# A two-layer decoder trunk: the RWKV pass over all tiles at once in two staggered halves, six projection units side by side at the start, and the 256-column matmul first in every second block

## The chip, the cores and the metric

The kernel runs on one core of a Trainium2 chip. The metric is the device time of one execution in microseconds (us); the kernel before took 2397.22 us as the median of three runs (2396.86 to 2416.54). "Within 1%" of that median is 2373.2 to 2421.2 us.

## The reference, cut to what matters

The input x is 256 tokens of 2048 features, float32. Two layers follow one another, each of the form

```python
h = _rms_norm(x, norm_mix[layer])
u = h @ w_in                       # one combined input projection
y = concat(head_group_1(u), head_group_2(u)) @ w_out
x = x + y
x = x + _sq_relu_mlp(_rms_norm(x, norm_mlp[layer]), w_ff1, w_ff2)   # 2048 -> 8192 -> 2048
```

In layer 0 the head groups are a sparse attention (NSA, 8 heads) and RWKV-7 time mixing (16 heads of 64), in layer 1 a gated linear recurrence and HGRN2. The change concerns the RWKV-7 recurrence, the projection ahead of it, and the way in which all the large products are issued. RWKV-7 is a recurrence over time with a 64x64 state per head:

```python
def step(state, inp):
    r_t, w_t, k_t, v_t, a_t, b_t = inp
    sa = jnp.einsum('bhij,bhj->bhi', state, a_t)
    state = state * w_t[:, :, None, :] + sa[..., None] * b_t[:, :, None, :] + v_t[..., None] * k_t[:, :, None, :]
    return state, jnp.einsum('bhij,bhj->bhi', state, r_t)
```

## The kernel before, in words

Activations lie transposed: 128 features on the partitions, 256 tokens along the free axis, 16 such tiles for 2048 features. Float32 accuracy on TensorE is had by splitting. An activation tile `hx[k]` is 512 columns wide: 256 columns of its rounded high part and 256 of the rest (`prepare`, L192). A weight tile is split in the same way by `split` (L128): a cast on ScalarE makes `wh` (L130), a subtraction on VectorE makes `wl` (L132), eight 128x128 tiles at a time. One product of a weight tile with an activation tile, called a block here, is then two matmuls (`mm3`, L147): `wh` against all 512 columns (L152) and `wl` against the 256 high columns (L153), both into one PSUM bank. A `unit` (L156) is 16 such blocks, k = 0 to 15, for 128 output features. Where only half the columns are wanted (`folded`, the second half of the output projection) the 512-column matmul is two of 256 columns (L149, L150), so a block is three matmuls of 256 columns.

There are 48 units in each input projection (`mm_i`), 64 up and 64 down units in each MLP (`mm_f`, 4096 blocks in all), and the output projections (`mm_o`) have 256 blocks in their first and 256 in their folded halves over both layers: 6144 blocks with the 1536 of the input projections. Weights stream from memory in 512 KB pieces on SP's queue (L125).

Layer 0's mix (`layer0_mix`, L233) goes in these steps:

- The start (L251 to L288): x and the first units' weights are loaded, `hx` is made tile by tile, then units 0 and 1 run one after the other, then 2 and 3.
- `rwkv_a` (L310): the rest of units 0 to 27. For each of eight tiles j (two heads each) it forms decays, keys, values and the 64x64 pair products, and stores them to memory: `rwp_d` (128 x 2052 per tile: the vectors `a`, `r`, the transposed keys and values, the decay, the bonus and the gate) and `pm_d` (pair products). All of these DMAs are on GpSimd's queue. From `pm_d` small 32x32 pieces are gathered into `nb` (L432).
- `rw_solve` (L437): 30 steps of two VectorE operations invert these triangles; the result goes to memory as `z_d` (L448).
- `rwkv_b` (L450): four passes, for the tile pairs (0,1), (2,3), (4,5), (6,7). A pass loads `inv` from `z_d`, `pm`, `rwp` and `bg` (L466 to L470), completes the inverse with two groups of 32x32 matmuls (`psh` L478, `psf` L484), then walks four chunks of 64 tokens: `psx` (state part L494 with 128 rows and 64 columns of TensorE, pair part L496 with 64 rows), copy, `psu` (L503, 64 rows), copy, new state `pss` (L510, 128x128), output `psy` (state part L521, 128x128; value part L523). At the end of a pass come a mean (`pmn`, L529), a variance (`pvr`, L534) and the result's halves in `yr` (L543, L544). `rwp` has one buffer, so a pass's load waits for the pass before it.
- `nsa_keys` and `nsa_head` (units 28 to 47 and the attention's small matmuls `nr_q`, `s`, `t`, `o`).
- `out_proj` (L917): first the half that reads `yr`, then, folded, the half that reads `yn`.

A scheduler sorts the instructions of each engine when the program is built, with the priorities that the code sets; on the chip each engine takes its list strictly in order. It lays matmuls of NSA heads and of units between the RWKV steps.

## Time and profile before

| | |
|---|---|
| median of 3 runs | 2397.22 us |
| lowest, highest | 2396.86, 2416.54 us |
| the profiled execution | 2415.31 us, of which the span is 2413.5 us |
| granted TensorE clock, mean of the span | 0.997 |
| busy: PE, DVE, ACT, POOL | 2390.6, 1697.7, 1243.7, 44.9 us |

The profiled execution is one of the two longer ones among the four times that are known, 18.1 us above the median. PE is TensorE (PEld its weight loads), DVE VectorE, ACT ScalarE, POOL GpSimd, SP the queue that loads the weights. Matmuls are pipelined and their ends are modelled, so that the distance between the starts of two matmuls tells what one costs, and not the duration that its row gives. A float32 matmul outside the split products stands as two instructions in the trace.

### The profile page before, as it was taken

Reading aid. Unit: us, or ns where it says so; the run is one execution under the profiler, and the core shown is the slowest. Engines: PE = TensorE matmul, PEld = TensorE weight load, DVE = VectorE, ACT = ScalarE, POOL = GpSimd, SP = SyncE. Lnnn points to the kernel's source line nnn. Section 1 sums busy time; section 2 is a strip of 40 time slices with the busy share of each in tenths; the row PEclk is TensorE's granted clock in tenths of the full one; section 3 lists DMA queues with packets and bytes.
Section 4 is the critical chain, followed back from the end, with each engine's and each line's share of the span. In section 5 each row is a group of like instructions: output and inputs, shape, how many; then the busy total and the mean of one; then the engine's idle time right before and its main releaser. Section 6 shows DMA issues by size and latency. Waiting matters only on the chain.

```text
span 2413.5 us, 37947 instructions
## 1 busy us (share of the span) xinstructions
PE 2390.6 (99%) x14386; PEld 2072.1 (86%) x14386; DVE 1697.7 (70%) x3006; ACT 1243.7 (52%) x2152; POOL 44.9 (2%) x118
## 2 busy tenths in 40 slices
PE   8999999999999999999999999999999999999999
PEld 6888877798888888888888888889888888888888
DVE  7887865677676576576568888788777667667555
ACT  7554455555444444444456666675544444444443
POOL 0112010000000000000000000000000000000000
PEclk9999999999999999999999999999999999999999
DMA  7667743465555555655555444456556555656564
GB/s 263 212 216 228 246 139 105 155 209 183 190 184 186 188 184 187 188 185 187 187 176 187 150 151 153 154 168 217 185 191 191 189 188 191 192 187 190 191 199 134
DMA packets 125862, 446.77 MB, mean 185 GB/s; under 512 B 14192, under 2 KB 19952, under 8 KB 124016
## 3 DMA queue, kind: packets, MB, share of 16 engines
q1 hardware_dynamic: 115824, 414.06, 53.7%
q0 software_dynamic: 5456, 26.79, 3.1%
q10 hardware_dynamic: 4400, 3.50, 0.4%
q8 instruction: 114, 1.87, 0.3%
q14 instruction: 68, 0.56, 0.1%
HBM read 429.06 MB, written 15.22 MB: 184 GB/s over the span
## 4 chain that ended last, share of the span: by engine, by line
PE 93%; DVE 3%; DMA 2%; ACT 1%; issue 1%; POOL 0%; DVEq 0%; ACTq 0%; POOLq 0%
PE mm_f L152 39%; PE mm_f L153 20%; PE mm_i L152 13%; PE mm_i L153 7%; PE mm_o L153 2%; PE mm_o L152 1%; PE mm_o L149 1%; PE mm_o L150 1%; DVE wl_i L132 1%; PE hl L816 1%; PE pair L425 1%; DMA rwp<-rwp_d 1%; PE psx L496 0%; ACT wh_o L130 0%; PE psu L503 0%
## 5 line engine op out<-in xcount | busy, mean ns | idle before, releaser
L132 DVE TENSOR_TENSOR wl_f<-raw_f,wh_f 128x1024 fp32r<-128x1024 f32 x512 | 627.2, 1225 | 486.1 <-ACT wh_f L130 486.1
L130 ACT CAST wh_f<-raw_f 128x1024 fp32r<-128x1024 f32 x512 | 538.6, 1052 | 773.4 <-PE mm_f L152 566.8
L152 PE MATMUL mm_f<-hx_m,wh_f 128*128 128x512 f32 x2048 | 717.2, 395 | 0.0
L152 PE MATMUL mm_f<-z,wh_f 128*128 128x512 f32 x2048 | 717.1, 395 | 0.0
L152 PE MATMUL mm_i<-hx_a,wh_i 128*128 128x512 f32 x1536 | 563.9, 405 | 11.5 <-ACT wh_i L130 11.4
L153 PE MATMUL mm_f<-hx_m,wl_f 128*128 128x256 f32 x2048 | 574.8, 281 | 0.0
L153 PE MATMUL mm_f<-z,wl_f 128*128 128x256 f32 x2048 | 574.4, 280 | 0.0
L152 PEld LDWEIGHTS mm_f<-z,wh_f 128*128 128x128 f32 x2048 | 383.9, 187 | 90.0
L152 PEld LDWEIGHTS mm_f<-hx_m,wh_f 128*128 128x128 f32 x2048 | 383.9, 187 | 90.0
L153 PE MATMUL mm_i<-hx_a,wl_i 128*128 128x256 f32 x1536 | 447.6, 291 | 1.2 <-DVE wl_i L132 1.0
L153 PEld LDWEIGHTS mm_f<-hx_m,wl_f 128*128 128x128 f32 x2048 | 387.0, 189 | 0.1
L153 PEld LDWEIGHTS mm_f<-z,wl_f 128*128 128x128 f32 x2048 | 387.0, 189 | 0.0
L152 PEld LDWEIGHTS mm_i<-hx_a,wh_i 128*128 128x128 f32 x1536 | 289.8, 189 | 72.3 <-ACT wh_i L130 12.1
L153 PEld LDWEIGHTS mm_i<-hx_a,wl_i 128*128 128x128 f32 x1536 | 291.5, 190 | 9.3 <-DVE wl_i L132 4.0
L130 ACT CAST wh_i<-raw_i 128x1024 fp32r<-128x1024 f32 x192 | 201.3, 1049 | 188.9 <-PE mm_i L152 169.5
L132 DVE TENSOR_TENSOR wl_i<-raw_i,wh_i 128x1024 fp32r<-128x1024 f32 x192 | 234.5, 1222 | 80.6 <-ACT wh_i L130 76.4
L168 DVE TENSOR_TENSOR s_f<-mm_f,t_f 128x256 f32<-128x256 f32 x256 | 106.7, 417 | 3.0 <-ACT t_f L167 3.0
L132 DVE TENSOR_TENSOR wl_o<-raw_o,wh_o 128x1024 fp32r<-128x1024 f32 x64 | 78.3, 1223 | 32.6 <-ACT wh_o L130 32.3
L130 ACT CAST wh_o<-raw_o 128x1024 fp32r<-128x1024 f32 x64 | 67.2, 1050 | 63.3 <-issue 29.2
L167 ACT COPY t_f<-mm_f 128x256 f32<-128x256 f32 x256 | 93.2, 364 | 4.3 <-PE mm_f L153 4.3
L153 PE MATMUL mm_o<-ym,wl_o 128*128 128x256 f32 x256 | 72.6, 284 | 0.8 <-DVE wl_o L132 0.8
L942 DVE TENSOR_TENSOR s_f<-s_f,rstd_m 128x256 f32<-128x256 f32 x128 | 54.4, 425 | 4.4
(420 smaller groups left out, 2254.7 us busy)
## 6 DMA issues: line engine op xcount, KB each, us to landing
raw_f<-in_w_ff_dram SPq DMA_DIRECT2D x512, 512.0 KB, 4.5
raw_i<-in_w_in_dram SPq DMA_DIRECT2D x192, 512.0 KB, 4.1
raw_o<-in_w_out_dram SPq DMA_DIRECT2D x64, 512.0 KB, 4.2
rwp_d<-rwp POOLq DMA_DIRECT2D x8, 1026.0 KB, 7.1
rwp<-rwp_d POOLq DMA_DIRECT2D x4, 1540.0 KB, 10.7
cw<-in_cmp_w_dram SPq DMA_DIRECT2D x2, 2048.0 KB, 10.2
...
```

The source lines that it names most:

```text
L130: A.copy(wh, raw)
L132: V.tensor_sub(wl, raw, wh)
L149: M.matmul(ps[:, :T], wh, mv[:, :T], start=first, stop=False)
L150: M.matmul(ps[:, :T], wh, mv[:, T:], start=False, stop=False)
L152: M.matmul(ps, wh, mv, start=first, stop=False)
L153: M.matmul(ps[:, :T], wl, mv[:, :T], start=False, stop=last)
L167: A.copy(t, ps[:, T:])
L168: V.tensor_add(s, ps[:, :T], t)
L425: M.matmul(pps[q][:, c * P : (c + 1) * P], bk[hs, c], ar[hs, c], start=True, stop=True)
L816: M.matmul(pl[:, x * T + i * P : x * T + (i + 1) * P], qk[:, ii], qk[:, ii], start=True, stop=True)
L942: V.tensor_mul(s, s, rstd)
```

## The change

Three things are changed, and what follows from them.

1. **Six units at the start.** `w_in0` is laid out so that for each k the 128x128 weight tiles of units 0 to 5 lie together (768 columns, 384 KB). For each k the loop makes `hx[k]`, splits the six tiles and issues six blocks into six PSUM banks. Sixteen matmuls on a zeroed tile stand ahead of the first block. The small loads of `rw_w2`, `rw_a2` and `rw_g2` wait for the first cast (`issue_after`).
2. **RWKV in one pass.** `rwkv_b` is called once and works in two halves of four tiles (eight heads) each. Per chunk of 64 tokens and half it loads `inv` (four DMAs), `pm`, `rw` and `gb` into two buffers that both halves share, zeroes the upper rows of the values in `rw` with a memset on GpSimd, and does all steps for four tiles at once. The pair parts of `psx` and `psu` now use all 128 rows of TensorE (with zeroed rows in `xv`, `inv` and `rw`), and the parts with the state and the state's update are split by head into 64 columns. Mean and variance are taken per chunk. The two halves are generators whose steps alternate, the first one four steps ahead. `rwp_d` and `pm_d` are one tensor each, by chunk.
3. **Turned blocks.** In `unit`, and in the first half of `out_proj`, every odd k issues the `wl` matmul ahead of the `wh` matmul. Units 0 to 5 and the folded half are not turned.

```diff
+NFIRST = 6
...
-    def mm3(ps, wh, wl, mv, first, last, folded=False):
+    def mm3(ps, wh, wl, mv, first, last, folded=False, turned=False):
+        if turned:
+            M.matmul(ps[:, :T], wl, mv[:, :T], start=False, stop=False)
+            M.matmul(ps, wh, mv, start=False, stop=last)
+            return
...
-            mm3(ps, wh[:, k % 8], wl[:, k % 8], mv[k], k == 0, k == KT - 1, folded)
+            mm3(ps, wh[:, k % 8], wl[:, k % 8], mv[k], k == 0, k == KT - 1, folded, k % 2 == 1)
...
+            rwp_d = dram.tile([P, 8, 4, 512], F32, name="rwp_d")
+            pm_d = dram.tile([P, 8, 4, 2, P], F32, name="pm_d")
+            wts = mx.tile([P, 8, 4], F32, name="wts", bufs=1)
...
+                w_k = w_in0[0:NFIRST].rearrange("n p m -> (n p m)").rearrange("(k p c) -> k p c", k=KT, p=P)
+                first = [
+                    pmm.tile([P, 512], F32, tag="mm", name=f"mm_i0_{u}") if u < 2 else bank(f"mm_i0_{u}", ("ga", "gb", "gc")[(u - 2) % 3])
+                    for u in range(NFIRST)
+                ]
+                wrm = pa.tile([P, P], F32, name="wrm")
+                V.memset(wrm, 0.0)
+                pw = bank("warm", "gc")
...
+                    for k in range(KT):
+                        if k % 2 == 0:
+                            nc.sync.dma_start(xi[k // 8][:, k % 8 : k % 8 + 2], xT[:, k : k + 2])
+                        raw = wraw.tile([P, 8, P], F32, tag="raw", name=f"raw_i0_f{k}")
+                        nc.sync.dma_start(raw[:, :NFIRST], w_k[k].rearrange("p (b c) -> p b c", c=P))
+                        raws.append(raw)
+                        if k == 9:
+                            nc.sync.dma_start(con, consts)
+                    for i in range(16):
+                        M.matmul(pw[:, :P], wrm, wrm, start=True, stop=True)
...
+                    for k in range(KT):
+                        prepare(hx, k, xi[k // 8][:, k % 8], "gmix0")
+                        wh = wspl.tile([P, 8, P], F32R, tag="wh", name=f"wh_i0_f{k}")
+                        ins = A.copy(wh[:, :NFIRST], raws[k][:, :NFIRST])
+                        anchor = anchor or ins.ins
+                        wl = wspl.tile([P, 8, P], F32R, tag="wl", name=f"wl_i0_f{k}")
+                        V.tensor_sub(wl[:, :NFIRST], raws[k][:, :NFIRST], wh[:, :NFIRST])
+                        for u in range(NFIRST):
+                            mm3(first[u], wh[:, u], wl[:, u], hx[k], k == 0, k == KT - 1)
+                        if k % 4 == 3:
+                            squares(k // 4)
+                    rstd = rstd_of(acc, "a0", "gc")
+                first.append(unit(w_in0[NFIRST], hx, f"i0_{NFIRST}", tag="gb"))
+                rwkv_a(pa, gate, hx, scaled_by(rstd), rwp_d, pm_d, wts, nb, first, load_cw, anchor)
             with tc.tile_pool(name="pb", bufs=1) as pb, tc.tile_pool(name="pn", bufs=1) as pn:
                 rw_solve(pb, nb, z_d)
...
-                for j in range(0, 8, 2):
-                    rwkv_b(pb, j, rwp_d, pm_d, z_d, yr)
+                rwkv_b(pb, rwp_d, pm_d, z_d, wts, yr)
...
+        inv_ = [tl(f"inv{i}", (P, 8, 64)) for i in range(2)]
+        xv_ = [tl(f"xv{i}", (P, 4, P)) for i in range(2)]
+        s_ = [tl(f"s{i}", (P, 4, P)) for i in range(2)]
+        for t in inv_ + xv_ + s_:
+            G.memset(t, 0.0)
+        zv = z_d.rearrange("(i j c q) r t -> i c q r j t", i=2, j=8, c=4)
...
+            for i in range(2):
+                for q in range(2):
+                    G.dma_start(inv8[32 * i : 32 * i + 32, :, q, 32 * i : 32 * i + 32], zv[i, c, q, :, js])
+            pm = tl("pm", (P, 4, 2, P), 2, name=f"pmc_{n_}")
+            G.dma_start(pm, pm_d[:, js, c])
+            rw = tl("rw", (P, 4, 384), 2, name=f"rw_{n_}")
+            G.dma_start(rw, rwp_d[:, js, c, 0:384])
+            gb = tl("gb", (P, 4, 128), 2, name=f"gb_{n_}")
+            G.dma_start(gb, rwp_d[:, js, c, 384:512])
+            G.memset(rw[0:64, :, 256:384], 0.0)
...
+            psx = bank(f"psx_{n_}")
+            for r in range(4):
                 if c:
-                    M.matmul(psx[0:64, r * P : (r + 1) * P], ar[:, r, c, 0], s[:, r], start=True, stop=False)
+                    M.matmul(psx[0:64, r * P : (r + 1) * P], ac[:, r], s[:, r], start=True, stop=False)
                 for h in range(2):
-                    M.matmul(psx[0:64, r * P + h * 64 : r * P + h * 64 + 64], pm[64:128, r, 4 * h + c, 0:64],
-                             uv[64:128, r, c, h * 64 : h * 64 + 64], start=c == 0, stop=c == 0 or h == 1)
+                    M.matmul(psx[0:64, r * P + h * 64 : r * P + h * 64 + 64], pm[:, r, h, 0:64],
+                             uv[:, r, h * 64 : h * 64 + 64], start=c == 0, stop=c == 0 or h == 1)
...
+                    M.matmul(psu[0:64, r * P + h * 64 : r * P + h * 64 + 64], inv[:, 2 * r + h],
+                             xv[:, r, h * 64 : h * 64 + 64], start=True, stop=True)
...
+                    o = psy[h * 64 : h * 64 + 64, r * 64 : r * 64 + 64]
+                    if c:
+                        M.matmul(o, s[:, r, h * 64 : h * 64 + 64], rc[:, r], start=True, stop=False)
+                    M.matmul(o, uv[:, r, h * 64 : h * 64 + 64], pm[:, r, h, 64:128], start=c == 0, stop=True)
...
+                        M.matmul(pss[h * 64 : h * 64 + 64, r * 64 : r * 64 + 64],
+                                 rw[:, r, 128 + h * 64 : 128 + h * 64 + 64], uv[:, r, h * 64 : h * 64 + 64], start=True, stop=True)
...
+        halves = [chain.from_iterable(map(chunk, range(4), [b] * 4)) for b in range(2)]
+        for _ in range(4):
+            next(halves[0])
+        while halves:
+            halves = [h for h in halves if next(h, 1) is None]
...
-                        mm3(ps, wh[:, k], wl[:, k], ym[half * 8 + k], k == 0, k == 7, o == 1)
+                        mm3(ps, wh[:, k], wl[:, k], ym[half * 8 + k], k == 0, k == 7, o == 1, o == 0 and k % 2 == 1)
```

The order of the instructions, as the scheduler lays them, changes at three places on which the prediction rests. First TensorE's list inside one unit of the first MLP (`mm_f1_0_0_1` is the unit's bank, `hx_m0` the activations, `wh` and `wl` the two parts of the weights), before and after:

```order
L152 MATMUL mm_f1_0_0_1_6222<-hx_m0_0_5108,wh_f1_0_0_1_0_6225 128x512
L153 MATMUL mm_f1_0_0_1_6222<-hx_m0_0_5108,wl_f1_0_0_1_0_6227 128x256
L152 MATMUL mm_f1_0_0_1_6222<-hx_m0_0_5108,wh_f1_0_0_1_0_6225 128x512
L153 MATMUL mm_f1_0_0_1_6222<-hx_m0_0_5108,wl_f1_0_0_1_0_6227 128x256
L152 MATMUL mm_f1_0_0_1_6222<-hx_m0_0_5108,wh_f1_0_0_1_0_6225 128x512
```

```order
L159 MATMUL mm_f1_0_0_1_6370<-hx_m0_0_5256,wh_f1_0_0_1_0_6373 128x512
L160 MATMUL mm_f1_0_0_1_6370<-hx_m0_0_5256,wl_f1_0_0_1_0_6375 128x256
L152 MATMUL mm_f1_0_0_1_6370<-hx_m0_0_5256,wl_f1_0_0_1_0_6375 128x256
L153 MATMUL mm_f1_0_0_1_6370<-hx_m0_0_5256,wh_f1_0_0_1_0_6373 128x512
L159 MATMUL mm_f1_0_0_1_6370<-hx_m0_0_5256,wh_f1_0_0_1_0_6373 128x512
```

Long and short matmuls alternated before; now two short ones and two long ones follow one another, and no matmul is added or lost.

Second TensorE's list in the second chunk of an RWKV pass. Before it is the group `psx` in chunk 1 of the pair (2,3); `st` is the state, `rwp` and `pm` are what the pass loaded:

```order
L494 MATMUL psx_2_1_2850<-st_2_0_2841,rwp_2_2778 64x128
L496 MATMUL psx_2_1_2850<-rwp_2_2778,pm_2_2777 64x64 x2
L494 MATMUL psx_2_1_2850<-st_2_0_2841,rwp_2_2778 64x128
L496 MATMUL psx_2_1_2850<-rwp_2_2778,pm_2_2777 64x64 x2
```

After it is the same group in chunk 1 of the first half (`s0` is its state, `rw` and `pmc` what it loads):

```order
L522 MATMUL psx_1_0_2853<-s0_2657,rw_1_0_2805 64x128
L524 MATMUL psx_1_0_2853<-rw_1_0_2805,pmc_1_0_2803 64x64 x2
L522 MATMUL psx_1_0_2853<-s0_2657,rw_1_0_2805 64x128
L524 MATMUL psx_1_0_2853<-rw_1_0_2805,pmc_1_0_2803 64x64 x2
L522 MATMUL psx_1_0_2853<-s0_2657,rw_1_0_2805 64x128
L524 MATMUL psx_1_0_2853<-rw_1_0_2805,pmc_1_0_2803 64x64 x2
L522 MATMUL psx_1_0_2853<-s0_2657,rw_1_0_2805 64x128
L524 MATMUL psx_1_0_2853<-rw_1_0_2805,pmc_1_0_2803 64x64 x2
```

One group now serves four tiles, and there are eight such groups for the kernel instead of sixteen. Between the first `psh` and the last `pvr` TensorE's list holds, beside the RWKV matmuls, 86 blocks and some seven NSA heads before, and 28 blocks and three heads after; what left that stretch stands behind it.

Third GpSimd's list where `rwkv_a` ends (`nb` is the gathering of the triangles for `rw_solve`, `pmc`, `rw` and `gb` the loads of the first chunk of the first half, `_0_0`, and of the second, `_0_1`). Before:

```order
L462 MEMSET inv_0_2599 64x1024
L468 DMA pm_0_2601<-pm_d0_99 128x2048
L469 DMA rwp_0_2602<-rwp_d0_95 128x2x1540
L470 DMA bg_0_2603<-rwp_d0_95 128x2x512
L432 DMA nb_105<-pm_d3_102 8x32x32 x2
```

After:

```order
L498 DMA pmc_0_0_2669<-pm_d_96 128x4x256
L500 DMA rw_0_0_2671<-rwp_d_95 128x4x384
L502 DMA gb_0_0_2673<-rwp_d_95 128x4x128
L498 DMA pmc_0_1_2733<-pm_d_96 128x4x256
L503 MEMSET rw_0_0_2671 64x4x128
L500 DMA rw_0_1_2735<-rwp_d_95 128x4x384
L502 DMA gb_0_1_2737<-rwp_d_95 128x4x128
L456 DMA nb_100<-pm_d_96 8x32x32
```

The last gathering into `nb` now stands behind a memset (L503) that has to wait until the first `rw` load has landed.

## Rows read from the trace of the kernel before

**Rows 1.** The page, part 1: busy us, share of the span and instructions of each engine.

```profile
PE 2390.6 (99%) x14386; PEld 2072.1 (86%) x14386; DVE 1697.7 (70%) x3006; ACT 1243.7 (52%) x2152; POOL 44.9 (2%) x118
```

**Rows 2.** The page, part 4: the chain that ended last, shares by engine.

```profile
PE 93%; DVE 3%; DMA 2%; ACT 1%; issue 1%; POOL 0%; DVEq 0%; ACTq 0%; POOLq 0%
```

**Rows 3.** Four windows: length, busy us and (count) of PE, PEld, DVE, ACT, POOL, clock, DMA, GB/s.

```profile
575.00:1275.00 700.00, 700.00 (x3964) 607.04 (x3963) 454.31 (x646) 321.31 (x461) 0.00 (x0) 1.00 0.58 185
1725.00:2375.00 650.00, 650.00 (x3752) 573.15 (x3751) 422.39 (x590) 296.29 (x413) 0.00 (x0) 1.00 0.60 192
316.60:459.50 142.90, 142.45 (x1167) 107.44 (x1168) 82.75 (x293) 76.01 (x222) 10.55 (x15) 0.96 0.33 112
322.00:325.00 3.00, 3.00 (x16) 2.14 (x16) 0.47 (x3) 1.92 (x8) 0.00 (x0) 0.50 0.04 11
```

**Rows 4.** The timeline of PE in layer 1's MLP: start us, us, instruction.

```profile
2000.30 0.39 PE L152 MATMUL mm_f<-hx_m,wh_f 128*128 128x512 f32 x1
2000.53 0.28 PE L153 MATMUL mm_f<-hx_m,wl_f 128*128 128x256 f32 x1
2000.65 0.39 PE L152 MATMUL mm_f<-hx_m,wh_f 128*128 128x512 f32 x1
```

**Rows 5.** The timeline of PE in the folded half of the output projection.

```profile
529.86 0.28 PE L149 MATMUL mm_o<-yn,wh_o 128*128 128x256 f32 x1
529.98 0.28 PE L150 MATMUL mm_o<-yn,wh_o 128*128 128x256 f32 x1
530.10 0.28 PE L153 MATMUL mm_o<-yn,wl_o 128*128 128x256 f32 x1
```

**Rows 6.** The chain in order of time, 250 to 480 us: start, us on it, what.

```profile
316.62 1.20 PE psh L478 x32
...
324.62 1.04 PE psu L503 x8
...
347.29 12.62 DMA rwp<-rwp_d
360.04 0.65 PE psx L496 x8
...
435.27 0.44 PE pss L510 x4
435.71 0.38 PE psy L523 x8
437.02 0.37 PE psx L496 x4
...
438.86 0.60 PE psu L503 x8
...
441.63 0.36 PE psy L521 x2
...
450.87 0.36 PE psx L494 x2
...
457.61 0.87 PE pvr L534 x2
```

**Rows 7.** The timeline of all engines at the start of the kernel.

```profile
6.05 2.90 ACT L193 ACTIVATE hx_a<-xi,par 128x256 fp32r<-128x256 f32 x7 [4.04 <-DMA xi<-in_xT_dram]
...
10.92 0.80 PE L152 MATMUL mm_i<-hx_a,wh_i 128*128 128x512 f32 x1 [10.92 <-ACT wh_i L130]
...
13.20 0.63 PE L152 MATMUL mm_i<-hx_a,wh_i 128*128 128x512 f32 x1
...
13.84 0.63 PE L152 MATMUL mm_i<-hx_a,wh_i 128*128 128x512 f32 x1
```

**Rows 8.** Window from 0 to 50.3 us, line L152 alone: length, PE, PEld, clock, DMA share, GB/s.

```profile
0.00:50.30 50.30, 35.76 (x96) 18.68 (x96) 1.00 0.80 277
```

**Rows 9.** Groups by line, 0 to 25 us: busy us, mean ns | idle before, releaser.

```profile
L194 DVE SCALAR_TENSOR_TENSOR hx_a<-xi,par,hx_a 128x256 fp32r<-128x256 f32 x16 | 6.5, 480 | 6.6 <-ACT hx_a L193 6.6
...
L132 DVE TENSOR_TENSOR wl_i<-raw_i,wh_i 128x1024 fp32r<-128x1024 f32 x5 | 6.0, 1220 | 1.5 <-ACT wh_i L130 1.4
```

More of the change, by code (lines that the diff above doesn't have):

```diff
@@ L2 @@
 from contextlib import ExitStack
+from itertools import chain
 import numpy as np
@@ L54 @@
 HG_LEVELS = (1, 2, 4, 8, 16, 32)
-RWP_N = 4 * 512 + 4
+NFIRST = 6
 @with_exitstack
@@ L235, in layer0_mix @@
             acc, hx = norm("a0")
-            rwp_d = [dram.tile([P, 2, RWP_N], F32, name=f"rwp_d{j}") for j in range(4)]
-            pm_d = [dram.tile([P, 2, 8, P], F32, name=f"pm_d{j}") for j in range(4)]
+            rwp_d = dram.tile([P, 8, 4, 512], F32, name="rwp_d")
+            pm_d = dram.tile([P, 8, 4, 2, P], F32, name="pm_d")
+            wts = mx.tile([P, 8, 4], F32, name="wts", bufs=1)
             z_d = dram.tile([P, 32, 32], F32, name="z_d")
@@ L316, in shifted @@
             G.memset(ub[:, 0:1], 0.0)
-            scaled(first[u] if u < 4 else unit(w_in0[u], hx, f"i0_{u}"), ub[:, 1:], name)
+            scaled(first[u] if u < len(first) else unit(w_in0[u], hx, f"i0_{u}"), ub[:, 1:], name)
             d = tl("d", bufs=2, name=f"d_{name}")
@@ new lines, in tl, with chunk @@
+            return pb.tile(list(shape), F32, tag=tag, name=name or tag, bufs=bufs)
+        inv_ = [tl(f"inv{i}", (P, 8, 64)) for i in range(2)]
[4 more added lines that the diff above has]
+        zv = z_d.rearrange("(i j c q) r t -> i c q r j t", i=2, j=8, c=4)
+        def chunk(c, b):
+            inv, xv, s = inv_[b], xv_[b], s_[b]
+            js = slice(4 * b, 4 * b + 4)
+            n_ = f"{c}_{b}"
+            inv8 = inv.rearrange("p (j q) t -> p j q t", q=2)
+            for i in range(2):
[8 more added lines that the diff above has]
+            G.memset(rw[0:64, :, 256:384], 0.0)
+            pm8 = pm.rearrange("p j q t -> p (j q) t")
+            zat = tl(f"zat{b}", (64, 8, 32), name=f"zat_{n_}")
+            V.transpose(zat[0:32], inv[0:32, :, 0:32])
+            psh = bank(f"psh_{n_}")
+            for n in range(8):
+                M.matmul(psh[32:64, n * 32 : (n + 1) * 32], pm8[0:32, n, 32:64], zat[0:32, n], start=True, stop=True)
+            A.copy(zat[32:64].rearrange("p n t -> p (n t)"), psh[32:64, 0:256])
+            yield
+            psf = bank(f"psf_{n_}")
+            for n in range(8):
+                M.matmul(psf[0:32, n * 32 : (n + 1) * 32], zat[32:64, n], inv[32:64, n, 32:64], start=True, stop=True)
+            A.copy(inv[0:32, :, 32:64], psf[0:32, 0:256].rearrange("p (n t) -> p n t", n=8))
+            ac, rc, uv = rw[:, :, 0:64], rw[:, :, 64:128], rw[:, :, 256:384]
+            yield
+            psx = bank(f"psx_{n_}")
+            for r in range(4):
@@ L517, in rwkv_b @@
-            psy = bank(f"psy_{j}_{c}")
-            for r in R:
-                rr = slice(r * 64, r * 64 + 64)
-                if c:
-                    M.matmul(psy[:, rr], s[:, r], ar[:, r, c, 1], start=True, stop=False)
-                for h in range(2):
-                    M.matmul(psy[h * 64 : h * 64 + 64, rr], uv[:, r, c, h * 64 : h * 64 + 64], pm[:, r, 4 * h + c, 64:128],
-                             start=c == 0, stop=True)
-            A.copy(y4[:, :, c], psy[:, 0:P].rearrange("p (r t) -> p r t", r=2))
@@ L526, in rwkv_b @@
-            s = sn
-        yf = y.rearrange("p r t -> p (r t)")
-        pmn = bank(f"pmn_{j}")
-        M.matmul(pmn, bones, yf, start=True, stop=True)
-        V.scalar_tensor_tensor(yf, pmn, -1.0 / 64, yf, ALU.mult, ALU.add)
-        sq = tl("ysq", (P, 512))
-        A.activation(sq, yf, AF.Square)
-        pvr = bank(f"pvr_{j}")
-        M.matmul(pvr, bones, sq, start=True, stop=True)
-        rs = tl("ysq", (P, 512), name=f"yrs_{j}")
-        rsqrt_of(rs, pvr, 1.0 / 64, eps_ln, f"y{j}", pb)
@@ new lines, in chunk @@
+            A.copy(xv[0:64].rearrange("p r t -> p (r t)"), psx[0:64])
+            yield
+            psu = bank(f"psu_{n_}")
+            for r in range(4):
+                for h in range(2):
+                    M.matmul(psu[0:64, r * P + h * 64 : r * P + h * 64 + 64], inv[:, 2 * r + h],
+                             xv[:, r, h * 64 : h * 64 + 64], start=True, stop=True)
+            A.copy(uv[0:64], psu[0:64].rearrange("p (r t) -> p r t", r=4))
+            yield
+            psy = bank(f"psy_{n_}")
@@ new lines, in chunk @@
+            yield
+            pmn = bank(f"pmn_{n_}")
+            M.matmul(pmn[:, 0:T], bones, y, start=True, stop=True)
+            V.scalar_tensor_tensor(y, pmn[:, 0:T], -1.0 / 64, y, ALU.mult, ALU.add)
+            sq = tl(f"ysq{b}", (P, T), name=f"ysq_{n_}")
+            A.activation(sq, y, AF.Square)
+            yield
+            pvr = bank(f"pvr_{n_}")
+            M.matmul(pvr[:, 0:T], bones, sq, start=True, stop=True)
+            rs = tl(f"ysq{b}", (P, T), name=f"yrs_{n_}")
+            rsqrt_of(rs, pvr[:, 0:T], 1.0 / 64, eps_ln, f"y{n_}", pb)
```

162 lines of the change are left out of this document (54 added, 108 removed).

## The prediction, made before the result was known

> **What bounds the kernel now.** I read the busy times first, then the chain that ended last, then windows by stage, and the timeline only where two windows disagreed. TensorE is busy for 99% of the span, the next engine, VectorE, for 70% [rows 1], and 93% of the chain that ended last is TensorE [rows 2]. So time is won where TensorE does less, goes from one matmul to the next faster, or stands still less. Busy alone does not tell these apart, so I count matmuls in windows. Layer 0's MLP issues 3964 matmuls in 700 us, which is 1982 blocks of 353.2 ns; layer 1's MLP, the same code, 3752 in 650 us, which is 1876 blocks of 346.5 ns [rows 3]. The program has two paces and stays in one for a whole MLP. The difference is 6.7 ns on 2048 blocks, 13.7 us. The profiled execution took 2415.3 us (span 2413.5 and 1.8 around it), 18.1 us more than the median. With the faster pace in layer 0's MLP it would have been 2401.6, and the input projections of layer 0 have stretches of the slow pace too, so I take the median of 2397.2 for a run at the fast pace throughout. The sum is made against 2415.3, and the 18.1 is taken off at the end.
>
> The RWKV passes are the stretch with the poorest use of TensorE. From the first `psh` at 316.6 us to the end of the last `pvr` at 458.5 [rows 6] four passes follow one another, 35.5 us each. PE counts as busy in all of it, while the DMA share falls to 0.33 [rows 3]: few weights are consumed.
>
> **Turned blocks.** Nothing is added; 2896 pairs of blocks change their order (2048 in the MLPs, 42 and 48 units with 8 each in the projections, 128 in the output projections). A pair was long, short, long, short; it becomes long, short, short, long. So of each pair one step from short to long and one from long to short go, and a step from short to short and one from long to long come. The trace shows long to short as 230 ns and short to long as 120 at two digits [rows 4], and short to short as 120 in the folded half [rows 5]. Long to long it does not show. The bare columns are 213.3 and 106.7 ns at 2.4 GHz, the level that the windows at 1.00 stand for [rows 3]. Short to short is thus its columns and 13.3 ns, and a block of 346.5 is its 320.0 ns of columns and 26.5, twice the same. I therefore take each matmul to cost its columns and 13.3 ns in any order, and long to long to cost 226.7: the change is 0. The bounds are the bare 213.3 and, as far on the other side, 240: the slow pace shows that at least 6.7 ns more are possible. That is 13.3 ns either way on 2896 pairs, 38.5 us down or up.
>
> **Six units at the start.** The first block begins at 10.92 us, after half a unit of weights and eight tiles of x [rows 7]. After the change it needs one k: the first activation tile can be made at 6.05 us as now [rows 7], in 0.5 us, and the cast of 768 columns follows, 0.8 us, so 7.4. But sixteen matmuls stand ahead of it. One float32 matmul of 128 columns is 0.22 us (two `pss` take 0.44 [rows 6]) and double that at half clock, so they take some 7 us from about 1 us on: 8.0. That is 2.9 us earlier. The first blocks now go 0.64 us apart [rows 7], not 0.35; seven of them cost 2.0 us, which the sixteen matmuls take over. From then on TensorE needs 6 x 0.347 = 2.08 us per k. VectorE needs 0.48 for the activation, 0.92 for 768 of the 1024 columns of 1220 ns [rows 9], and about 0.4 for the squares, 1.8 together. The loads are 512 KB per k, 252 GB/s, and the first 50 us ran at 277 [rows 8]. Both fit with little to spare, so I give 1.9 of the 4.9 us back for misses. Now 96 blocks are reached at 50.3 us [rows 8]; the small matmuls that ran between them come later and cost what they cost. Term: -3 us, between -5 and +2.
>
> **RWKV in one pass.** The cost of TensorE's groups is read from the chain [rows 6]. Before, one chunk with a state, for two tiles: `psx` 2 x (0.36 + 0.37) = 1.46, `psu` 0.60, `pss` 0.44, `psy` 2 x 0.36 + 0.38 = 1.10, together 3.60. Chunk 0 has no state: 0.65 + 0.60 + 0.44 + 0.38 = 2.07. Chunk 3 has no `pss`: 3.16. With 2.3 for `psh` and `psf` (1.20, taken alike) and 1.75 for `pmn` and `pvr` (0.87, alike), a pass is 2.07 + 7.20 + 3.16 + 4.05 = 16.5, and four are 66 us.
>
> After, one chunk of one half serves four tiles. Four pair matmuls of `psx` in one form take 0.65 and two take 0.37 [rows 6]: 0.14 for each and 0.09 once per group. With the same form throughout, `psx` is 8 x 0.14 + 4 x 0.22 + 0.09 = 2.1 and `psu` 8 x 0.14 + 0.09 = 1.2. `psy` (16 matmuls) and `pss` (8) alternate between the two column positions as L523 does, 0.095 each: 1.5 and 0.8. `psh` and `psf` are 1.15, mean and variance 0.9. That is 7.65; chunk 0 is 6.0 and chunk 3 6.9. A half is 6.0 + 15.3 + 6.9 = 28.2, both 56.4. Term: -9.6 us. Bounds: nothing gained (all 0.14 and a switch at each group), and -17 (all at 0.095).
>
> The row for `psx` is where a rule can be weighed: two matmuls of L496 between two of L494 take 0.37, four together 0.65, so that four in pieces would take 0.74 [rows 6]. The Trainium skill, TensorEngine Tiling (Array Packing), Key Properties, says that a change of the tiling mode drains TensorE; the trace agrees in sign, with 0.09 us. By that rule the one form inside a chunk is a gain, but each NSA or projection matmul laid between the groups still pays it.
>
> The waits around this work I leave as they are: 141.9 us of wall time held 66 of RWKV work, and what else stood there (86 blocks and seven heads) moves behind the stretch, where the `yr` half of the output projection fills between the heads. What a chunk loads is new on the path. The longest load that ended the chain is 12.62 us, once [rows 6]; that wait can go, or six later chunk loads can each show 4 us of theirs, since both halves share two buffers: between -12 and +24. I take 0, because 81 us of TensorE work (56.4, 28 blocks and three heads of 5 us) stand between the groups. VectorE and ScalarE, 83 and 76 us busy in that 143 us window [rows 3], have room.
>
> The last gathering into `nb` stands behind a memset that waits for a load of the RWKV values, the like of which took 12.62 us [rows 6]. `rw_solve` starts later, while TensorE's list reaches the first `psh` 12 matmuls earlier, 12 x 0.173 = 2.1 us. Between 0 and +12; I take +2.
>
> **Sum.** 2415.3 - 3.0 - 9.6 + 2.0 = 2404.7 for the profiled pace; less 18.1, 2386.6, so 2386 us for the median.
>
> **The rivals.**
>
> *A long matmul after a long one costs its bare columns.* Then 13.3 ns go on 2896 pairs, 38.5 us: 2347. For it: the weights of the second long matmul have twice the time of the short one to arrive, and the 120 of short to short may come from them. Against it: a long matmul costs 230 though the weights of the short one that follows had the same long time [rows 4]. The opposite, 240, would be 2425.
>
> *The slow pace holds.* If the new order falls into the slow pace in one MLP, as layer 0's does here [rows 3], the median is 2386 + 13.7 = 2400. The trace shows that both occur with the same code; it does not show what chooses.
>
> *Half clock in the RWKV pass.* This is the way to a slower kernel. Inside the first pass the clock stands at 0.50 (322 to 325 us [rows 3]), when 32x32 matmuls and waits had gone before, and `psu` takes 1.04 us there and 0.60 later [rows 6], 1.7 times as long. After, the 81 us of this stretch hold only 28 blocks of full-size matmuls instead of 86. If all of it ran at half clock, 57 us more: 2443. Each us at half clock loses 0.41, so it takes 35 us of loss, 85 us at half clock, to be slower than before by over 1%. Against it: passes two to four hold the same matmuls, and the mean of all 142.9 us is still 0.96 [rows 3].
>
> **How the numbers follow.** My forecast has 0.44; its own range by the bounds above is 2362 to 2400, and about 0.13 of the 0.44 lies under 2373.2. The bare long matmul has 0.27, of which 0.25 lies under 2373.2. The slow pace has 0.16, all within 1%. Half clock, long loads in the RWKV pass, or a dearer long matmul have 0.13, of which 0.11 lies above 2421.2. A measurement here can tell about 1% from no change. So faster by over 1%: 0.38; within: 0.51; slower: 0.11. The range reaches from the first rival's 2347, with part of the RWKV gain beside it, 2338, to the slow pace with some load waits, 2412.
>
> **What would show it right or wrong.** In the windows over the two MLPs: 346.5 ns per block with turned blocks, and about 227 from long to long on the timeline. A block near 340 is the first rival, near 353 the second. The first block at 8 us, and 96 blocks by about 44. From the first `psh` to the last `pvr` 75 to 100 us; the granted clock there; `rw` loads on the chain for less than 20 us. The forecast is wrong if the MLPs' blocks change by over 3 ns, or if the RWKV stretch and what follows it, up to the first MLP matmul, do not end about 10 us earlier.

## The result and the profile after

The changed kernel took 2427.1 us (median of 7 runs, 2425.2 to 2430.4), the kernel before, run beside it, 2398.6 (7 runs); the ratio is 1.010, 95% interval 1.007 to 1.013. The forecast was 2386 us with a range up to 2412: the time is 41 us above the forecast. Runs of the kernel before stand in two groups, at about 2397 and 2411 us, a distance that fits the two paces of its MLPs [rows 3], and its profile is of the upper group; stages are therefore compared in the profiles.

The profiled execution took 2426.5 us (span 2424.7). Its stages, from the starts of TensorE's matmuls in the traces; run 1 is the first experiment below, which has the first two parts of the change without turned blocks:

| us | before | after | run 1 |
|---|---|---|---|
| start to the first matmul of layer 0's MLP | 559.0 | 540.8 | 537.7 |
| layer 0's MLP | 724.2 | 728.7 | 710.6 |
| layer 1's mix and output projection | 415.0 | 422.0 | 415.0 |
| layer 1's MLP | 710.6 | 728.7 | 710.7 |

The first row is 18 us shorter, some 4 us of which are the slower execution that was profiled before (18.1 us above the median, 13.6 of it in layer 0's MLP). Both MLPs, which only the turned blocks touch, lose the gain and more against the quick pace of 710.6. Part 1 of the page, after, still calls PE busy for 99%, as [rows 1]:

```profile
PE 2403.2 (99%) x14530; PEld 2045.1 (84%) x14530; DVE 1718.2 (71%) x3031; ACT 1260.5 (52%) x2148; POOL 70.1 (3%) x164
```

What changed stands in the idle column of part 5 (busy us, mean ns | idle us before, and what ended most of it), after:

```profile
L174 ACT COPY t_f<-mm_f 128x256 f32<-128x256 f32 x256 | 95.4, 373 | 469.0 <-PE mm_f L153 469.0
...
L160 PEld LDWEIGHTS mm_f<-hx_m,wl_f 128*128 128x128 f32 x1024 | 192.4, 188 | 86.8 <-DVE wl_f L135 47.9
...
L160 PEld LDWEIGHTS mm_f<-z,wl_f 128*128 128x128 f32 x1024 | 192.2, 188 | 52.5 <-DVE wl_f L135 2.4
```

The same lines of run 1, without turned blocks:

```profile
L160 PEld LDWEIGHTS mm_f<-hx_m,wl_f 128*128 128x128 f32 x2048 | 387.1, 189 | 0.1
...
L174 ACT COPY t_f<-mm_f 128x256 f32<-128x256 f32 x256 | 92.9, 363 | 4.3 <-PE mm_f L160 4.3
```

Two things are new. ScalarE spends 469 us waiting in front of `t_f`, the eviction copy, where it waited 4. This is a sign of another order and no loss in itself: in run 1 ScalarE waits in front of the cast `wh_f` instead, 759.0 us against 258.7 after. And the weight loads of `wl_f` in the up units (operand `hx_m`) wait 48 us for VectorE's subtraction, those of the down units (`z`) hardly at all. The eviction copies tell the time of a unit, since there is one in each: the summary of L174 in layer 1's MLP, 1740 to 1835 us (up) and 1900 to 1960 us (down), gives the first and the last start. After:

```profile
L174 ACT COPY t_f<-mm_f x16: 373/373/373, 1744.5 to 1831.5; 128x256 f32<-128x256 f32 x16
...
L174 ACT COPY t_f<-mm_f x11: 372/373/373, 1900.4 to 1956.2; 128x256 f32<-128x256 f32 x11
```

Up units stand 87.0 / 15 = 5.80 us apart (362.5 ns per block), down units 55.8 / 10 = 5.58 (348.7). From the starts of all matmuls: 5800 and 5577 ns in both layers, against 5547 for the quick pace of before (346.7 ns per block). So 128 up units lose 0.223 us to something that the down units don't meet, 28.5 us, and all 256 units lose 0.030, 7.7 us. With 7.0 us in layer 1's mix that is 43 of the 46 us between after and run 1; the other 3 stand ahead of layer 0's MLP.

The timelines show the 0.223. TensorE in an up unit of layer 1, after (H, the long matmul, is L159 or L153; L, the short one, L160 or L152; [rows 4] show plain blocks):

```profile
2004.27 0.40 PE L153 MATMUL mm_f<-hx_m,wh_f 128*128 128x512 f32 x1
2004.50 0.40 PE L159 MATMUL mm_f<-hx_m,wh_f 128*128 128x512 f32 x1
2004.85 0.38 PE L160 MATMUL mm_f<-hx_m,wl_f 128*128 128x256 f32 x1
2005.07 0.28 PE L152 MATMUL mm_f<-hx_m,wl_f 128*128 128x256 f32 x1
2005.19 0.39 PE L153 MATMUL mm_f<-hx_m,wh_f 128*128 128x512 f32 x1
```

The weight loads there:

```profile
2004.85 0.19 PEld L160 LDWEIGHTS mm_f<-hx_m,wl_f 128*128 128x128 f32 x1 [0.40 <-DVE wl_f L135]
2004.96 0.19 PEld L152 LDWEIGHTS mm_f<-hx_m,wl_f 128*128 128x128 f32 x1
2005.08 0.19 PEld L153 LDWEIGHTS mm_f<-hx_m,wh_f 128*128 128x128 f32 x1
```

ScalarE and VectorE of the same unit:

```profile
2001.91 0.37 ACT L174 COPY t_f<-mm_f 128x256 f32<-128x256 f32 x1 [1.92 <-PE mm_f L153]
2002.18 1.06 ACT L133 CAST wh_f<-raw_f 128x1024 fp32r<-128x1024 f32 x1
...
2002.32 0.42 DVE L175 TENSOR_TENSOR s_f<-mm_f,t_f 128x256 f32<-128x256 f32 x1 [1.06 <-ACT t_f L174]
2002.78 0.43 DVE L979 TENSOR_TENSOR s_f<-s_f,rstd_m 128x256 f32<-128x256 f32 x1
2003.23 0.42 DVE L980 SCALAR_TENSOR_TENSOR s_f<-s_f 128x256 f32<-128x256 f32 x1
2003.58 1.22 DVE L135 TENSOR_TENSOR wl_f<-raw_f,wh_f 128x1024 fp32r<-128x1024 f32 x1
```

The matmul at 2004.50 is the ninth block's, the first of the unit's second half. Its L comes 0.35 us later instead of 0.23, and the next L 0.22 instead of 0.12: 0.22 in all. Read backwards: the load waits for a subtraction that ends at 2004.80; that began at 2003.58 though its cast was done at 2003.24, because the three eviction instructions stand ahead of it; and the cast itself began at 2002.18, behind `t_f`, which could begin only when the unit before had ended. The engines' lists, as built, say the same. ScalarE before:

```
L130 CAST wh_f1_1_1_15_1_19376<-raw_f1_1_1_15_1_19374 128x1024
L167 COPY t_f1_1_1_14_19359<-mm_f1_1_1_14_19314 128x256
```

ScalarE after:

```
L174 COPY t_f1_1_1_14_19507<-mm_f1_1_1_14_19462 128x256
L133 CAST wh_f1_1_1_15_1_19524<-raw_f1_1_1_15_1_19522 128x1024
```

`t_f1_1_1_14` evicts unit 14, `wh_f1_1_1_15_1` is the second half of unit 15. The buffer that this cast fills holds weights of unit 14, and is free once that unit's last H has read them. Before, an L came behind that H, and the scheduler put the cast ahead of the eviction; with the sixteenth block turned, the last H is the unit's end, and the eviction goes first. It does so at all 254 places where one MLP unit follows another in a layer, and the cast goes first at all 254 before.

The down units have the same order and don't wait, since their eviction has two instructions on VectorE and not three. After:

```profile
1906.25 1.06 ACT L133 CAST wh_f<-raw_f 128x1024 fp32r<-128x1024 f32 x1
...
1906.84 0.43 DVE L987 TENSOR_TENSOR xs<-xs,s_f 128x256 f32<-128x256 f32 x1
1907.34 1.23 DVE L135 TENSOR_TENSOR wl_f<-raw_f,wh_f 128x1024 fp32r<-128x1024 f32 x1
```

VectorE is through with the eviction at 1907.27 and the cast with `wh_f` at 1907.31, so the subtraction starts 0.03 us behind its cast, where it is 0.34 us late in the up unit.

The Trainium skill, TensorE: Matmul & The Clock Gate, section LDWEIGHTS (loading the stationary operand), gives a weight load in ns as its columns over 1.2, an estimate of 107 ns for 128. The trace agrees in the spacing: the three late loads start 0.11 and 0.12 us apart, though the row of each lasts 0.19. An L's bare columns are 106.7 ns, so by that rule a short matmul has nothing to spare for the load of the one behind it, and a load that came late under one short matmul is still late at the next.

### The profile page after: what moved, and what is told of

Read it like the earlier page. It is cut to its first block, busy times and chain, and to the rows that moved or that the text cites. A ratio compares the mean times of both kernels' runs of the same rounds, so it can differ in the third digit from the quotient of the medians.

```text
span 2424.7 us, 38016 instructions
## 1 busy us (share of the span) xinstructions
PE 2403.2 (99%) x14530; PEld 2045.1 (84%) x14530; DVE 1718.2 (71%) x3031; ACT 1260.5 (52%) x2148; POOL 70.1 (3%) x164
## 4 chain that ended last, share of the span: by engine, by line
PE 91%; DVE 3%; DMA 3%; ACT 2%; issue 1%; POOL 0%; SPq 0%; ACTq 0%; POOLq 0%; DVEq 0%
PE mm_f L153 20%; PE mm_f L159 20%; PE mm_f L160 11%; PE mm_f L152 10%; PE mm_i L159 6%; PE mm_i L153 5%; PE mm_i L160 3%; PE mm_i L152 3%; PE mm_o L160 2%; PE mm_o L157 1%; PE mm_o L156 1%; DVE wl_i L135 1%; PE mm_o L153 1%; PE mm_o L159 1%; PE hl L853 1%
## 5 line engine op out<-in xcount | busy, mean ns | idle before, releaser
L133 ACT CAST wh_f<-raw_f 128x1024 fp32r<-128x1024 f32 x512 | 540.9, 1056 | 258.7 <-PE mm_f L153 242.3
L159 PE MATMUL mm_f<-hx_m,wh_f 128*128 128x512 f32 x1024 | 405.2, 396 | 0.0
L153 PE MATMUL mm_f<-z,wh_f 128*128 128x512 f32 x1024 | 405.1, 396 | 0.0
L159 PE MATMUL mm_f<-z,wh_f 128*128 128x512 f32 x1024 | 404.8, 395 | 0.0
L153 PE MATMUL mm_f<-hx_m,wh_f 128*128 128x512 f32 x1024 | 404.7, 395 | 0.0
L174 ACT COPY t_f<-mm_f 128x256 f32<-128x256 f32 x256 | 95.4, 373 | 469.0 <-PE mm_f L153 469.0
L160 PE MATMUL mm_f<-hx_m,wl_f 128*128 128x256 f32 x1024 | 297.5, 291 | 0.0
L159 PE MATMUL mm_i<-hx_a,wh_i 128*128 128x512 f32 x720 | 294.2, 409 | 0.0
L153 PE MATMUL mm_i<-hx_a,wh_i 128*128 128x512 f32 x720 | 290.8, 404 | 0.0
L152 PE MATMUL mm_f<-z,wl_f 128*128 128x256 f32 x1024 | 285.2, 279 | 0.0
L152 PE MATMUL mm_f<-hx_m,wl_f 128*128 128x256 f32 x1024 | 285.0, 278 | 0.0
L160 PE MATMUL mm_f<-z,wl_f 128*128 128x256 f32 x1024 | 284.8, 278 | 0.0
L160 PEld LDWEIGHTS mm_f<-hx_m,wl_f 128*128 128x128 f32 x1024 | 192.4, 188 | 86.8 <-DVE wl_f L135 47.9
L135 DVE TENSOR_TENSOR wl_i<-raw_i,wh_i 128x1024 fp32r<-128x1024 f32 x180 | 219.8, 1221 | 35.2 <-ACT wh_i L133 33.8
L160 PEld LDWEIGHTS mm_f<-z,wl_f 128*128 128x128 f32 x1024 | 192.2, 188 | 52.5 <-DVE wl_f L135 2.4
L133 ACT CAST wh_i<-raw_i 128x1024 fp32r<-128x1024 f32 x180 | 189.0, 1050 | 83.1 <-PE mm_i L153 67.7
L152 PEld LDWEIGHTS mm_f<-hx_m,wl_f 128*128 128x128 f32 x1024 | 192.4, 188 | 41.2
L152 PEld LDWEIGHTS mm_f<-z,wl_f 128*128 128x128 f32 x1024 | 192.2, 188 | 41.1
L160 PE MATMUL mm_i<-hx_a,wl_i 128*128 128x256 f32 x720 | 212.2, 295 | 5.3 <-DVE wl_i L135 4.8
L152 PE MATMUL mm_i<-hx_a,wl_i 128*128 128x256 f32 x720 | 208.6, 290 | 0.0
```

The source lines that it names most:

```text
L133: A.copy(wh, raw)
L135: V.tensor_sub(wl, raw, wh)
L152: M.matmul(ps[:, :T], wl, mv[:, :T], start=False, stop=False)
L153: M.matmul(ps, wh, mv, start=False, stop=last)
L159: M.matmul(ps, wh, mv, start=first, stop=False)
L160: M.matmul(ps[:, :T], wl, mv[:, :T], start=False, stop=last)
```

## The experiments

**Four runs to place the loss.** Theory: the list order causes the wait. Rival 1: the order of the matmuls costs it by itself. Rival 2: the first two parts lose the time. Run 1 calls `mm3` without `turned` in `unit` and `out_proj`.

> No block is turned; the six units at the start and the RWKV part in one pass stay. Theory (a list order: with the unit's last matmul a long one, ScalarE's list has the eviction t_f ahead of the cast of the next unit's second half, VectorE's has the eviction's three instructions ahead of the subtraction, and TensorE waits 222 ns at the ninth block of the 128 up units, 28.4 us; and besides a turned pair costs 31 ns more per unit, 7.9 us over 256 units): both go, with some 3 to 5 us more in the mixes, so 2384 to 2390 us if both MLPs run at 347 ns per block, some 2400 if layer 0 holds 353 ns. Rival 1 (the order of the matmuls itself costs all of it): the same time. Rival 2 (the six units or the RWKV pass lose the time): 2415 us or more.

Measured 2380.7 us (2379.8 to 2381.3), ratio to before 0.992 (0.989 to 0.995); 5547 ns per unit in both MLPs. Rival 2 is out: parts 1 and 2 make the kernel faster, and the turned blocks cost 46 us. With run 12 below it is the quickest kernel here, and the one to keep. Run 2 adds `turned` alone to the kernel before.

> The kernel before with the turned blocks alone. Theory and rival 1: the MLPs take 362.5 ns per block in the up passes and 348.6 in the down passes as after the whole change, so 2398 + 36 + some 4 in the mixes, about 2438 us. Rival 2: no more than 2405 us.

Measured 2446.5 us, ratio 1.020 (1.016 to 1.023), up units 5800 and down units 5577 ns; layer 1's mix 422.3 us. That is 8 us more than expected in all, but the MLPs are as expected: the loss doesn't need the other parts. Run 3:

```diff
-            mm3(..., k == KT - 1, folded, k % 2 == 1)
+            mm3(..., k == KT - 1, folded, k % 2 == 1 and k < KT - 1)
```

> After, with every second block turned except a unit's last: each unit ends with a short matmul, and ScalarE's list has the cast ahead of the eviction again, as before the change. Theory: the wait at the ninth block goes, the up units take the 5578 ns of the down units or up to 4 ns less, and the time falls by 28 us to about 2399 us. Rival 1 (matmul order itself; 7 of 8 turned blocks stay, the one at the middle of the unit among them): up units at 5770 ns or more, about 2422 us.

Measured 2396.1 us, ratio 0.998 (0.995 to 1.000); up and down units alike, 5593 ns in layer 0 and 5587 in layer 1, some 10 to 15 more than expected. L174 from 1740 to 1835 us (89.4 / 16 = 5.59):

```profile
L174 ACT COPY t_f<-mm_f x17: 365/366/366, 1744.9 to 1834.3; 128x256 f32<-128x256 f32 x17
```

Seven of eight turned blocks stay, the cast goes first again at all 254 places, and the wait is gone. Run 4 leaves TensorE's order in the MLPs alone:

```diff
-        with tc.high_priority():
+        with tc.high_priority(40):
             A.copy(t, ps[:, T:])
```

> After, with all turned blocks as they are and only the eviction's priority lowered, so that ScalarE's list has the cast of the second half ahead of t_f and VectorE's the subtraction ahead of the eviction. Theory: TensorE's order is the same, the wait goes, up units at 5578 ns, about 2399 us. Rival 1: nothing changes in the up units (5800 ns), about 2427 us.

Measured 2405.0 us, ratio 1.001 (0.999 to 1.004). L174 from 1740 to 1835 us:

```profile
L174 ACT COPY t_f<-mm_f x17: 362/363/363, 1743.7 to 1832.8; 128x256 f32<-128x256 f32 x17
```

VectorE's timeline in a unit, where the subtraction now comes first:

```profile
2005.73 1.23 DVE L135 TENSOR_TENSOR wl_f<-raw_f,wh_f 128x1024 fp32r<-128x1024 f32 x1 [1.27 <-ACT wh_f L133]
2006.87 0.42 DVE L175 TENSOR_TENSOR s_f<-mm_f,t_f 128x256 f32<-128x256 f32 x1
```

Up units take 89.1 / 16 = 5.57 us: with the same MLP matmuls in the same order, only the cast and the subtraction ahead of the eviction, the wait is gone. Rival 1 falls for the 28 us. The two MLPs together are 29.6 us shorter than after; the stretch up to layer 0's MLP is 9.1 us longer, so that the span falls by 20. Of the 9.1, some 5 stand in the RWKV pass, where the granted clock from 318 to 400 us was 0.96 instead of 1.00, and some 5 behind it; TensorE's order differs there too, and the cause is open.

**Which block does it.** Run 7 turns every second block but the eighth (`k % 2 == 1 and k != 7`), run 8 none but the last of each unit (`k == KT - 1`; `out_proj` plain).

> After, with every second block turned except the eighth, the one in front of the place where TensorE waits; the last block of a unit stays turned, and ScalarE's list has the eviction ahead of the cast as after the change. Theory (list order): the wait at the ninth block of the up units stays, 200 ns or more of it, and the time is within 6 us of 2427 us. Rival 4 (the wait comes of the two short matmuls or the late release of the first half's slots around the middle of the unit): it goes, about 2399 us.

Measured 2421.7 us (two runs), up units 5800 ns. The wait stands, as the list order wants it; rival 4 is out.

> The run without turned blocks, with one change: the last block of each unit of 16 (one block in 16, in the input units and the MLPs) is turned, so that the unit ends with a long matmul; every other block is plain and two long matmuls stand side by side once a unit. ScalarE's and VectorE's lists then have the eviction ahead of the second half's cast and subtraction, as after the change. Theory (list order): most of the cost is back from this one block: the up units take 5547 + some 220 = 5770 ns, the down units 5547 to 5560, so 28 us on 2381, and some 4 us in the mixes, about 2410 us. Rival 1 (matmul order): 1/8 of the 46 us, about 2387 us.

Measured 2428.2 us, ratio 1.012 (1.010 to 1.014), as slow as eight turned blocks per unit, and 18 us more than expected. L174, the same two windows:

```profile
L174 ACT COPY t_f<-mm_f x16: 373/373/373, 1743.7 to 1831.2; 128x256 f32<-128x256 f32 x16
...
L174 ACT COPY t_f<-mm_f x11: 373/373/374, 1900.5 to 1956.5; 128x256 f32<-128x256 f32 x11
```

5.83 us and 5.60. The wait at the ninth block accounts for 0.2 of the 0.286 that an up unit loses. The rest, and the 0.053 of a down unit, lie in plain blocks: in the first half of a down unit they come in a pattern of three, 1060 ns long, which is 353.3 ns per block, the slower pace of before [rows 3], and in the second half at 346.7. One turned block per unit seemed to set off the slow pace. That became the next question.

**What sets off the slower pace.** Runs 9 and 10 turn one single block of the whole program, the fourth or the eighth of unit 17 of layer 0's 128:

```diff
-            mm3(..., k == KT - 1, folded)
+            mm3(..., k == KT - 1, folded, name == "f1_0_1_0" and k == 3)
```

> The run without turned blocks, with one single block turned in the whole program: the fourth block of the 17th of layer 0's 128 MLP units; the lists of the other engines are the same. Theory 5 (TensorE has two paces for plain blocks, 346.7 and 353.3 ns, and a pair of long matmuls throws it into the slower one, where it stays): the units behind it in layer 0 take 5653 ns in place of 5547, for 111 units 11.8 us, or up to the next wait of TensorE; about 2392 us. Rival 5 (only the turned pair itself costs, a few ns): layer 0 at 5547 ns throughout, 2381 us.

Measured 2393.3 us (8 runs), against 2380.7 without the block. Totals of runs 1 and 9 to 13 can't be compared more closely than to some 6 us: the stretch up to layer 0's MLP, with the same list of TensorE in all of them, took 536.8 to 542.4 us in their profiles. The pace is therefore read in the MLP. L174 of layer 0 from 560 to 627 us, ahead of the block, and from 740 to 1240 us, behind it:

```profile
L174 ACT COPY t_f<-mm_f x12: 367/367/367, 562.2 to 623.2; 128x256 f32<-128x256 f32 x12
...
L174 ACT COPY t_f<-mm_f x89: 363/366/368, 741.8 to 1239.3; 128x256 f32<-128x256 f32 x89
```

61.0 / 11 = 5.55 us per unit ahead of it, 497.5 / 88 = 5.65 behind it, to the end of the layer. Layer 1 runs at 5547 ns again. The timeline at the block:

```profile
628.61 0.28 PE L160 MATMUL mm_f<-hx_m,wl_f 128*128 128x256 f32 x1
628.73 0.28 PE L152 MATMUL mm_f<-hx_m,wl_f 128*128 128x256 f32 x1
628.85 0.40 PE L153 MATMUL mm_f<-hx_m,wh_f 128*128 128x512 f32 x1
629.08 0.39 PE L159 MATMUL mm_f<-hx_m,wh_f 128*128 128x512 f32 x1
629.31 0.28 PE L160 MATMUL mm_f<-hx_m,wl_f 128*128 128x256 f32 x1
629.43 0.40 PE L159 MATMUL mm_f<-hx_m,wh_f 128*128 128x512 f32 x1
629.66 0.28 PE L160 MATMUL mm_f<-hx_m,wl_f 128*128 128x256 f32 x1
629.78 0.40 PE L159 MATMUL mm_f<-hx_m,wh_f 128*128 128x512 f32 x1
```

The pair itself is not dear (0.12, 0.12, 0.23, 0.23); the plain blocks that follow are 0.35 or 0.36 apart instead of 0.347.

> The same with the eighth block of that unit turned in place of the fourth, so that the pair stands where the operands of the unit's second half first come in. Theory 5: 5653 ns behind it as with the fourth block, about 2392 us. Rival 5: 5547 ns, 2381 us.

Measured 2395.6 us; 5653 ns behind the block. Where in the unit it stands makes no difference. A turned block makes two L and two H neighbours; runs 11 and 12 part them. Run 11 passes `folded` for the one block (the H as two of 256 columns: four short ones in a row), run 12 issues its `wl` matmul over all 512 columns (three long ones in a row).

> The run without turned blocks, with one single block in the program cut otherwise: the fourth block of the 17th unit of layer 0's MLP has its 512-column matmul as two of 256 columns, so that four short matmuls stand in a row there and no two long ones. Theory 6 (short matmuls in a row throw TensorE into the slower pace): 5653 ns per unit behind it up to the layer's end, about 2393 us. Rival 6 (long after long does): 5547 ns throughout, about 2381 us.

> The same with the fourth block's 256-column matmul widened to 512 columns (it adds the small product that the kernel leaves out), so that three long matmuls stand in a row there and no two short ones. Theory 6: 5547 ns throughout, about 2381 us. Rival 6: 5653 ns behind it, about 2393 us.

Measured 2394.8 us (8 runs) and 2379.4 us (3 runs). L174 from 740 to 1240 us, run 11:

```profile
L174 ACT COPY t_f<-mm_f x89: 363/366/368, 740.3 to 1237.9; 128x256 f32<-128x256 f32 x89
```

Run 12:

```profile
L174 ACT COPY t_f<-mm_f x90: 366/366/367, 744.0 to 1237.7; 128x256 f32<-128x256 f32 x90
```

497.6 / 88 = 5.65 and 493.7 / 89 = 5.55. Short matmuls in a row set off the slower pace; three long ones in a row do not. Run 13 has the turned block of run 9 and, sixteen units later, the long one of run 12.

> The run without turned blocks, with two single blocks in layer 0's MLP changed: the fourth block of the 17th unit is turned (two short and two long matmuls in a row), and the fourth block of the 33rd unit has its 256-column matmul widened to 512 columns (three long matmuls in a row; it adds the small product that the kernel leaves out). Theory 7 (a long matmul in place of a short one lets TensorE fall back into the quick pace, as a short in place of a long throws it out): units 18 to 33 at 5653 ns, those behind at 5547, 1.7 us in all, about 2382 us. Rival 7 (the slower pace ends only where TensorE's stream of blocks ends): 5653 ns up to the layer's end, about 2393 us.

Measured 2392.3 us (8 runs); 5653 ns up to the end of the layer (the copy is L178 here):

```profile
L178 ACT COPY t_f<-mm_f x89: 363/366/368, 740.0 to 1237.6; 128x256 f32<-128x256 f32 x89
```

Theory 7 falls: a long run doesn't bring the quick pace back.

The starts of the MLPs tell where the slow pace comes from when no block is turned, as in layer 0 before. Run 1, layer 0:

```profile
537.49 0.28 PE L157 MATMUL mm_o<-yn,wh_o 128*128 128x256 f32 x1
537.61 0.28 PE L160 MATMUL mm_o<-yn,wl_o 128*128 128x256 f32 x1
537.73 0.40 PE L159 MATMUL mm_f<-hx_m,wh_f 128*128 128x512 f32 x1
...
540.57 0.39 PE L159 MATMUL mm_f<-hx_m,wh_f 128*128 128x512 f32 x1
540.97 0.70 PE L213 MATMUL ms_m<-acc_m,con 128*128 128x256 f32 x2
```

The first eight blocks, 537.73 to 540.57, take 354 ns each, right behind the folded half of the output projection, which is short matmuls alone. So it is in both layers of all nine profiles whose MLPs have plain blocks there (before and runs 1, 5, 6, 9 to 13). In the ninth block the norm's matmul `ms_m` stands between, which makes it 1.05 to 1.08 us long. Behind it the pace is 346.7 in both layers, but for layer 0 of the kernel before and of run 5, where it stays at 353.3. The order is that of run 11, short ones in a row and the slow pace behind them; no run changed the folded half. What decides whether the pace ends there, and what ends it inside a down unit of run 8, stays open.

**The first two parts apart.** Run 5 has the six units alone, run 6 the RWKV pass alone.

> The kernel before with the six units at the start alone. Theory (the RWKV pass carries most of what the two parts together gave, 20 us, since its matmuls take 51.6 us of TensorE in the run without turned blocks where they took 68.0 before): 3 to 5 us off, about 2396 us. Rival 3 (the start carries it and the pass gave its forecast 7 to 10 us): about 2389 us.

> The kernel before with the RWKV part in one pass alone. Theory: 16 us off, about 2385 us, and the RWKV matmuls at about 52 us of TensorE. Rival 3: 7 to 10 us off, about 2392 us.

Measured 2395.9 us, ratio 0.999 (0.997 to 1.002), and 2388.2, ratio 0.996 (0.994 to 0.999). Both medians mix the two paces of layer 0's MLP; the medians of the lower groups are 2396.7 (before, 13 runs of 19), 2394.1 (6 of 10) and 2387.1 (7 of 10): 2.6 and 9.6 us off, where run 1, with both, is 16 off. (One run of 2404.4 is in neither group of the kernel before.) TensorE's time for the RWKV groups, from start to start, is 68.0 us before, 54.0 in run 6 and 51.6 in run 1. Six units alone can't be told from no change, as the theory had it; the pass carries most, but its 9.6 us is what rival 3 expected and well short of the theory's 16, so that neither holds as it stood. That both together give some 4 us more than their sum lies within the 6 us by which the stretch ahead of the MLP varies.

## Why the prediction was wrong

**Turned blocks, "the change is 0".** This step failed, by 46 us. It counted matmuls and the steps between them, and these steps were about right: the pair of run 9 costs within some 4 ns what a plain pair costs, and the 0.23 from long to long (2004.27 to 2004.50) lies inside the bounds 213.3 to 240. What it did not ask was who waits for the last matmul of a unit. The step read one engine's list; the casts and subtractions for the next unit stand in the lists of ScalarE and VectorE, and run 4 shows that their order alone carries 28 to 30 us. The sum has no term for these engines in the MLPs. They have room in the mean: VectorE is 71% busy after. But a unit's second half had about 0.2 us to spare (a subtraction 0.34 us late made TensorE's matmul 0.12 us late), and the three eviction instructions ahead of the subtraction take 1.27 us.

**The slow pace.** It was a rival with 0.16, priced at 13.7 us for one MLP, and the text said that the trace does not show what chooses. The price was right: in run 9 it is 106 ns on each of 111 units, 11.8 us. That the change itself would set it off was not considered as the likely case. With a turned block in nearly every pair the pace is neither of the two, 348.3 to 349.6 ns (runs 3 and 4, and the down units after); why is open. It costs 7.7 us of the 46. The 7 us in layer 1's mix come with the turned blocks too (runs 1 and 2). Most of them hang on a unit's last block: the mix takes 417.3 us in run 3, where only that one is plain, and 419.2 in run 8, where only that one is turned, against 415.0 and 422.0. But in run 4 it still takes 422.2, so the cause there is open.

**The bare long matmul** (2347 us, 0.27) is refuted: long to long takes 0.23, not 0.213. Nor did the dearer one, 240 ns, come, though the 2425 us that the text gave for it is close to the result.

**Six units, -3.** About right, as far as run 5 can tell: 2.6 us. The first block begins at 6.74 us (8.0 forecast; 10.92 before [rows 7]), in TensorE's timeline after:

```profile
6.74 0.71 PE L159 MATMUL mm_i<-hx_a,wh_i_f 128*128 128x512 f32 x2
```

The 96th begins at 42.9 (44 forecast; 50.3 before [rows 8]), by the window of L159 after:

```profile
0.00:43.20 43.20, 33.27 (x96) 17.73 (x96) 1.00 0.83 270
```

**RWKV pass, -9.6, with `nb` +2.** Right in sign and place; 7.6 forecast, 9.6 measured alone. The groups of TensorE were 16.4 us shorter in run 1 instead of 9.6: 68.0 before, where the sum had 66, and 51.6, where it had 56.4. The term that was most mis-sized is `psy`, taken as 0.095 us for each of 16 matmuls; run 1's chain shows chunk 0's eight matmuls (16 instructions) in 0.62:

```profile
338.76 0.62 PE psy L541 x16
```

That is 0.077 each, and all of `psy` is 7.8 us where the sum had about 10.6. Load waits, taken as 0, stayed small: from the first `psh` to the last `pvr` it took 78 us (75 to 100 forecast), and on the chain of after, of the chunks' loads behind the first, one of `pmc` stands there, and none of `rw` (12.62 us before [rows 6]):

```profile
351.72 4.76 DMA pmc<-pm_d
```

**Half clock** (2443 us) did not come for the whole stretch: the window over it shows a granted clock of 0.98 in run 1 and of 1.00 after. It came for a part of it in others. From 318 to 400 us the clock was 0.98 in runs 1 and 12, 0.96 in 9 and 10, and 0.94 in 11 and 13; the stretch up to layer 0's MLP took 537.7 and 536.8, 538.2 and 542.2, 542.4 and 542.0 us. So this rival goes, roughly, with the spread of about 5 us, and not with the loss. Run 1:

```profile
320.00:399.00 79.00, 78.40 (x1035) 64.98 (x1036) 46.94 (x163) 46.56 (x129) 29.63 (x48) 0.98 0.49 154
```

After:

```profile
323.00:402.00 79.00, 77.70 (x1042) 64.44 (x1043) 45.69 (x158) 45.18 (x126) 29.68 (x48) 1.00 0.48 153
```

The sum without its failed term, 2386.6, stands 6 us above run 1's 2380.7. The slower result came from a path that no rival described, and the range ended 15 us short of it.
